# Streamed tiles at one offset within 256 bytes, weight sums on VectorE in the order of need, six raw buffers, and a ScalarE copy of one PSUM bank, in a two-layer diffusion backbone

## The chip, the core and the metric

The kernel runs on one core of a Trainium2 chip. The metric is the device time of one execution in microseconds (us). In what follows PE is the matrix engine (TensorE), PEld its weight loads, DVE is VectorE, ACT is ScalarE, POOL is GpSimd, and SP is the engine whose queue issues most of the DMAs.

## The reference

Two layers over 512 latent tokens x and 256 context tokens, width 1024. Each layer modulates and normalises, projects once, mixes tokens in three branches, gates and projects back, and ends in a SwiGLU feed-forward block (FFN) of hidden width 2816:

```python
for i in range(DEPTH):                      # DEPTH = 2
    hx = modulate(x, norm1_gain[i], mod_x[0], mod_x[1])
    zx = hx @ w_in[i]                       # 1024 -> q, k, v, pool, gating, 3 gates
    ...
    x = x + mod_x[2] * mixer_merge(zx, attn_x, *layer)
    x = x + mod_x[5] * swiglu(modulate(x, norm2_gain[i], mod_x[3], mod_x[4]),
                              w_ffn_in[i], w_ffn_out[i])
    if not last:                            # the context stream, same weights
        cx = cx + mod_c[2] * mixer_merge(zc, attn_c, *layer)
        cx = cx + mod_c[5] * swiglu(modulate(cx, ...), w_ffn_in[i], w_ffn_out[i])
return rmsnorm(x, final_gain)

def swiglu(h, w_in, w_out):
    gu = h @ w_in
    return (jax.nn.silu(gu[..., :D_FF]) * gu[..., D_FF:]) @ w_out
```

The outputs are fp32.

## The kernel before

**Matmuls.** Activations lie transposed in SBUF, features on the partitions and tokens along the free dimension. A fp32 product is made of three reduced-precision ones. Each operand is split into a high part and the rest: ACT writes the high part (names with `h`, as `wh_fo`), DVE the low part (`wl_fo`), and PE runs wh with the high activations, wl with the high ones and wh with the low ones (L321 to L323, and L1077 to L1079 in `product`). Raw weights come by DMA from SP's queue into 4 KB buffers (`rawp`, five of them), the split parts go to `hlp`. A matmul's operands stand in the profile as output, then moving activations, then weights. Moving operands are 512 columns wide for the x stream, 256 for the context stream, and 384 in the first layer's FFN.

**The first layer's FFN** (class `Seven`) takes both streams together, 768 tokens in two halves of 384. It uses a seven-product scheme for 2x2 blocks: the blocks of the activations are combined once into seven tiles B11, B21, T2, T1, T3, B22 and T4 (`norm`, `combine`; each split by ACT at L1022 and by DVE at L1023), and for each of 22 column pairs j of the weights DVE or POOL builds the sums S3, S1, S2 and S4 of the four weight blocks (L1098, L1100, L1102, L1104; S1, S2 and S4 are written over the raw tiles). A pair runs in four stages, A to D, each with its own split weights (`sg`, `sb`, `sc`, `su`):

- A: bank P gets B11, bank S gets B21. ACT copies P to m.
- B: P += T2, and ACT copies it to m6; bank R gets T1, and ACT copies it to m5.
- C: P += T3, and DVE adds it into m5 (L1188); R += B22, and DVE adds it into m6 (L1190).
- D: P += T4; the products of the halves become the hidden tile `fa` (L1197 to L1200).

A product is 12 matmuls of 384 columns. `chunk` follows every few pairs: the down projection into `pfo`, which DVE adds into X (L1221).

**Order.** The instructions of each engine are put in order by the tile framework from the order of the Python code, and each engine works through its own list. `Pipeline` keeps weight preparations two stages ahead of the matmuls that use them. Pairs 0 to 2 are begun early: their A products run while the other token half is still being normalised (`norm`, whose reciprocal root `rs_n2h` is a POOL instruction, L360, and whose row sums `ps_rbh` come from PE, L1033); for pairs 0 and 1 the four sums are POOL work, issued in `prep_a`. The FFN of the second layer and the mixers are ordinary matmuls on the `act` tiles; columns of the next layer's modulation (`mac`, `mq`, L250 to L253) are filled in between.

**Buffers.** Pools take SBUF in the order in which they are opened, so the size of each pool sets where the next one begins.

Of the kernel before, what the change touches and what calls it, by code (L numbers as in the profile page):

```python
# [19 lines left out]
P = 128  # L20
# [30 lines left out]
def hybrid_dit_kernel(ctx, tc, I, out):  # L51
# [4 lines left out]
    rawp = ctx.enter_context(tc.tile_pool(name="rawp", bufs=5))  # L56
    hlp = ctx.enter_context(tc.tile_pool(name="hlp", bufs=3))
    tmp = ctx.enter_context(tc.tile_pool(name="tmp", bufs=8))
    macp = ctx.enter_context(tc.tile_pool(name="macp", bufs=1))
    sml = ctx.enter_context(tc.tile_pool(name="sml", bufs=4))  # L60
    act = att = None
# [12 lines left out]
    def open_keys(l):  # L74
        nonlocal att
        kkp = zone("kkp", 1, "right")
        KK[:] = [kkp.tile([P, 2, CTX + SEQ], F32R, name=f"KK{l}{g}") for g in range(2)]
        att = zone("att", 2, "right")
# [327 lines left out]
    vtm = cst.tile([P, NT // P, P], F32, name="vtm")  # L406
# [579 lines left out]
    class Pipeline:  # L986
# [11 lines left out]

        def step(self):
            self.fill()  # L1000
            if not self.ready:
                return False
            do, w = self.ready.popleft()
            do(w)
            return True
# [3 lines left out]
    class Seven:  # L1009
# [38 lines left out]
        def combine(self):  # L1048

            b11, b21, b12, b22 = self.t  # L1050
            T2 = self.fap.tile([P, 4, HT], F32, tag="fa", name="T2")
            self.combo("T2")
            for h in (slice(0, 2), slice(2, 4)):
                V.tensor_tensor(b11[:, h], b12[:, h], b11[:, h], ALU.subtract)
                V.tensor_tensor(T2[:, h], b22[:, h], b11[:, h], ALU.subtract)
                self.split("T2", T2[:, h], h.start, h.stop)
                yield
            self.combo("T1")
            self.split("T1", b11, 0, 4)
            yield  # L1060
            V.tensor_tensor(b12, b22, b12, ALU.subtract)
            self.combo("T3")
            self.split("T3", b12, 0, 4)
            yield
            self.combo("B22")
            self.split("B22", b22, 0, 4)
            yield
            V.tensor_tensor(b21, b21, T2, ALU.subtract)
            self.combo("T4")
            self.split("T4", b21, 0, 4)  # L1070
# [10 lines left out]
        def pair(self, j, A, early=None):  # L1081
# [10 lines left out]
            def sums(which, eng=V):  # L1092
                g, u = d["g"], d["u"]
                a11, a12, a21, a22 = g[:, 0:4, :], g[:, 4:8, :], u[:, 0:4, :], u[:, 4:8, :]
                for x in which:
                    if x == 3:
                        d["S3"] = self.sp.tile([P, 4, P], F32, tag="S3", name=f"S3{j}")
                        eng.tensor_tensor(d["S3"], a11, a21, ALU.subtract)  # L1098
                    elif x == 1:
                        eng.tensor_tensor(a21, a21, a22, ALU.add)  # L1100
                    elif x == 2:
                        eng.tensor_tensor(a11, a21, a11, ALU.subtract)  # L1102
                    else:
                        eng.tensor_tensor(a12, a12, a11, ALU.subtract)  # L1104
# [12 lines left out]
            def prep_a():  # L1117
# [6 lines left out]
                elif early < 2:  # L1124
                    sums((3, 1, 2, 4), G)
                return w

            def prep_b():
                if early == 2:
                    sums((3, 1, 2))  # L1130
                w = parts("sb", d["g"][:, 0:4, :], d["u"][:, 0:4, :])
                if early in (None, 2):
# [3 lines left out]
            def prep_c():  # L1136
                return parts("sc", d["S3"], d["g"][:, 4:8, :])
# [48 lines left out]
            def run_c(w):  # L1186
                self.product(d["P"], w, 0, "T3", False)
                V.tensor_tensor(d["m5"], d["P"], d["m5"], ALU.add)  # L1188
# [16 lines left out]
    def ffn_seven(sv, streams, l, finish, mods):  # L1205
# [7 lines left out]
        def hidden(j):  # L1213
            t = sv.fap.tile([P, 2, NT], F32R, tag="fa", name=f"fa{l}{j}")
# [89 lines left out]
    rsc = cst.tile([P, 2], F32, name="rsc")  # L1304
# [3 lines left out]
    G.tensor_tensor(rsc, vc, half_neg[:, :2], ALU.pow)  # L1308
# [3 lines left out]
    def last_first(one, acc):  # L1312

        for i in range(2):
# [9 lines left out]
            if i == 0:  # L1324
                close("att", "kkp")
                seven.fap = zone("fap", 6, "right")
# [18 lines left out]
    seven.sp = zone("sp", 2)  # L1345
# [26 lines left out]
    pipe.fill(2)  # L1372
    for _ in range(3):
        pipe.step()
    run(seven.nx)
    cm = seven.combine()
    seven.late[0][0]()
    steps(cm, 2)
    for m, _ in seven.late[1:]:
        m()  # L1380
    for _, g in seven.late:
        g()
    run(cm)
    while pipe.step():
        pass
    close("sp", "cbp")
# [168 lines left out]
```

## Time and profile before

| | |
|---|---|
| median of 3 runs | 2111.31 us (2106.1 to 2111.85) |
| the profiled execution's own time | 2110.22 us |
| its span, first to last instruction | 2108.2 us |
| PE busy | 2014.7 us, 96% |
| PEld busy | 1721.2 us, 82% |
| DVE busy | 1287.2 us, 61% |
| ACT busy | 820.5 us, 39% |
| POOL busy | 444.7 us, 21% |
| mean granted TensorE clock | 0.986 |
| HBM traffic | 227.4 MB, 108 GB/s |

Busy time is the time in which an engine has at least one instruction at work; matmuls are pipelined, so two that follow each other overlap in the records, and the pace is read from start to start. The span lies 2.0 us under the run's own time. The clock is given as a share of 2.4 GHz, so 0.5 is 1.2 GHz.

### The profile page before, as it was taken

The page shows a single profiled execution, that of the slowest core. Times are in us where ns is not written, and L with a number is a line of the kernel's source. Part 1 is how long each engine was busy: PE and PEld are TensorE (multiplying, and loading weights), DVE is VectorE, ACT ScalarE, POOL GpSimd, SP SyncE. Part 2 cuts the span into 40 slices and gives each one's busy share as a digit, 9 for nine tenths or more (in the row PEclk, how much of TensorE's full clock was granted, in tenths as well). Part 3 has the DMA queues.
Part 4 walks back from the last instruction along what each step waited for, and adds up shares of the span by engine and source line. Part 5 has one row for each costly group of instructions (what it writes and reads, how often), then busy time and mean ns, then how long its engine had stood idle before and what let it go on. Part 6 is the DMA issues. An engine that isn't in the chain of part 4 may idle for free.

```text
span 2108.2 us, 28931 instructions
## 1 busy us (share of the span) xinstructions
PE 2014.7 (96%) x11423; PEld 1721.2 (82%) x11423; DVE 1287.2 (61%) x2014; ACT 820.5 (39%) x1400; POOL 444.7 (21%) x361
## 2 busy tenths in 40 slices
PE   6998999999999789999999999999999999999998
PEld 5988988777778779898989898777777788888886
DVE  4879628576774787665757545776755663343435
ACT  3655525343443534242525235453522342222223
POOL 3436302023773311010102012301211230000000
PEclk9999999999999899999999999999999999999999
DMA  9755733232553032232323123414246543333331
GB/s 299 212 162 158 209 90 94 66 100 69 177 165 110 11 110 70 85 94 68 95 60 110 52 89 91 115 51 125 61 125 195 170 120 102 98 90 99 92 94 47
DMA packets 326727, 233.47 MB, mean 111 GB/s; under 512 B 7680, under 2 KB 300720, under 8 KB 326592
## 3 DMA queue, kind: packets, MB, share of 16 engines
q1 hardware_dynamic: 323072, 226.78, 35.8%
q0 software_dynamic: 3280, 4.76, 1.1%
q8 instruction: 90, 1.47, 0.3%
q14 instruction: 45, 0.37, 0.1%
q10 hardware_dynamic: 240, 0.08, 0.0%
HBM read 225.30 MB, written 2.10 MB: 108 GB/s over the span
## 4 chain that ended last, share of the span: by engine, by line
PE 76%; DVE 13%; DMA 4%; issue 3%; ACT 3%; POOL 1%; ACTq 0%; POOLq 0%; DVEq 0%; SPq 0%
PE pfo L321 2%; PE pfo L323 2%; PE pP L1077 2%; PE pfo L322 2%; PE pP L1078 2%; PE pP L1079 2%; PE pfg1x L323 2%; PE pg1x L321 2%; PE pfu1x L323 2%; PE pfu1x L322 2%; PE pfu1x L321 2%; PE pfg1x L321 2%; PE pfg1x L322 2%; PE pg1x L322 2%; PE pg1x L323 2%
## 5 line engine op out<-in xcount | busy, mean ns | idle before, releaser
L251 POOL TENSOR_TENSOR mac<-mac,mq 128x512 f32<-128x512 f32 x84 | 133.6, 1590 | 270.5 <-ACT mq L250 266.8
L253 DVE SCALAR_TENSOR_TENSOR mac<-wm,scv,mac 128x512 f32<-128x512 f32 x140 | 132.4, 945 | 11.6 <-DMA wm<-in_w_mod_dram 9.3
L321 PE MATMUL pfo<-fa,wh_fo 128*128 128x512 f32 (+1 forms) x288 | 99.4, 348 | 9.7 <-DVE X L1221 9.5
L323 PE MATMUL pfo<-fa,wh_fo 128*128 128x512 f32 (+1 forms) x288 | 97.2, 338 | 0.0
L322 PE MATMUL pfo<-fa,wl_fo 128*128 128x512 f32 (+1 forms) x288 | 97.1, 337 | 0.0
L303 ACT ACTIVATE wh_fo<-raw_fo 128x1024 fp32r<-128x1024 f32 (+1 forms) x44 | 44.8, 1019 | 115.3 <-issue 111.2
L1221 DVE SCALAR_TENSOR_TENSOR X<-pfo,modv,X 128x256 f32<-128x256 f32 (+1 forms) x80 | 48.1, 614 | 62.2 <-PE pfo L323 61.8
L304 DVE TENSOR_TENSOR wl_fo<-raw_fo,wh_fo 128x1024 fp32r<-128x1024 f32 (+1 forms) x44 | 53.7, 1222 | 47.6 <-ACT wh_fo L303 47.4
L360 POOL TENSOR_TENSOR rs_fin<-v_fin,half_neg 128x1 f32<-128x1 f32 x4 | 3.1, 773 | 365.1 <-DVE v_fin L358 365.1
L321 PE MATMUL pg0x<-n1x0h,wh_g0x 128*128 128x512 f32 x192 | 76.3, 397 | 1.1 <-ACT tg0x L812 1.1
L322 PE MATMUL pg0x<-n1x0h,wl_g0x 128*128 128x512 f32 x192 | 76.0, 396 | 0.9 <-DVE wl_g0x L304 0.9
L321 PE MATMUL pg1x<-n1x1h,wh_g1x 128*128 128x512 f32 x192 | 76.9, 400 | 0.0
L322 PE MATMUL pg1x<-n1x1h,wl_g1x 128*128 128x512 f32 x192 | 76.3, 398 | 0.0
L323 PE MATMUL pg1x<-n1x1l,wh_g1x 128*128 128x512 f32 x192 | 76.2, 397 | 0.0
L323 PE MATMUL pg0x<-n1x0l,wh_g0x 128*128 128x512 f32 x192 | 75.8, 395 | 0.0
L321 PE MATMUL pfg1x<-n2x1h,wh_fg 128*128 128x512 f32 (+1 forms) x184 | 71.5, 388 | 0.8 <-ACT n2x1h L390 0.8
L323 PE MATMUL pfg1x<-n2x1l,wh_fg 128*128 128x512 f32 (+1 forms) x184 | 71.5, 388 | 0.5 <-POOL n2x1l L391 0.3
L321 PE MATMUL pfu1x<-n2x1h,wh_fu 128*128 128x512 f32 (+1 forms) x184 | 71.0, 386 | 0.0
L322 PE MATMUL pfu1x<-n2x1h,wl_fu 128*128 128x512 f32 (+1 forms) x184 | 70.9, 386 | 0.0
L322 PE MATMUL pfg1x<-n2x1h,wl_fg 128*128 128x512 f32 (+1 forms) x184 | 70.9, 385 | 0.0
L323 PE MATMUL pfu1x<-n2x1l,wh_fu 128*128 128x512 f32 (+1 forms) x184 | 70.9, 385 | 0.0
L321 PEld LDWEIGHTS pfo<-fa,wh_fo 128*128 128x128 f32 x288 | 54.3, 189 | 19.8 <-DVE X L1221 13.2
(799 smaller groups left out, 6589.0 us busy)
## 6 DMA issues: line engine op xcount, KB each, us to landing
wm<-in_w_mod_dram SPq DMA_DIRECT2D x96, 512.0 KB, 4.5
raw_fo<-in_w_ffn_out_dram SPq DMA_DIRECT2D x40, 512.0 KB, 3.4
raw_g0c<-in_w_in_dram SPq DMA_DIRECT2D x24, 512.0 KB, 4.6
raw_g0x<-in_w_in_dram SPq DMA_DIRECT2D x24, 512.0 KB, 3.8
raw_g1x<-in_w_in_dram SPq DMA_DIRECT2D x24, 512.0 KB, 4.0
raw_g<-in_w_ffn_in_dram SPq DMA_DIRECT2D x22, 512.0 KB, 4.0
raw_u<-in_w_ffn_in_dram SPq DMA_DIRECT2D x22, 512.0 KB, 4.0
raw_fg<-in_w_ffn_in_dram SPq DMA_DIRECT2D x22, 512.0 KB, 3.9
```

Of the source, the lines that this page charges most:

```text
L251: G.tensor_tensor(a, a, q, ALU.add)
L253: V.scalar_tensor_tensor(a, raw[:, k, :], sck, a, ALU.mult, ALU.add)
L303: S.activation(wh, raw_ap, AF.Copy)
L304: (eng or V).tensor_tensor(wl, raw_ap, wh.bitcast(F32), ALU.subtract)
L321: T_.matmul(ps, wh, H, start=first, stop=False)
L322: T_.matmul(ps, wl, H, start=False, stop=False)
L323: T_.matmul(ps, wh, L, start=False, stop=last)
L360: G.tensor_tensor(rs, v, half_neg[:, :nb], ALU.pow)
L1077: T_.matmul(ps, wh[:, k0 + k, :], H, start=first and k == 0, stop=False, skip_group_check=True)
L1078: T_.matmul(ps, wl[:, k0 + k, :], H, start=False, stop=False, skip_group_check=True)
L1079: T_.matmul(ps, wh[:, k0 + k, :], L, start=False, stop=k == 3, skip_group_check=True)
L1221: V.scalar_tensor_tensor(x, ps, modv[l][:, 40 + n, s.r:s.r + 1], x, ALU.mult, ALU.add)
```

## The change

**Buffer addresses.** The pool of small tiles is opened first; `rawp` has six buffers for five and `tmp` nine for eight; the tile `vtm` moves from the constants into the zone of the keys; `rsc` grows from 2 to 50 floats and a tile `line` of 192 bytes is added ahead of the `mac` tiles; the hidden tiles are divided over two zones, `fap` with four buffers and `fbp` with two. In the built programs the pools of matmul operands begin at these bytes of a partition (remainder by 256 in brackets), and every tile in them is a multiple of 256 bytes long:

| tiles | before | after |
|---|---|---|
| raw weights (`rawp`) | 35744 (160) | 33248 (224) |
| split weights (`hlp`) | 56224 to 76704 (160) | 57824 to 78304 (224) |
| `mac` tiles | 97696 (160) | 101600 (224) |
| activations and FFN blocks (`act`, `cbp`) | 102176 (32) | 105696 (224) |
| hidden tiles (`fap`, after also `fbp`) | (224) | (224) |
| keys | 217056 (224) | 217056 (224) |

So between a matmul's moving operand and its weights there were 128 bytes (modulo 256) in most matmuls and 64 in those of the first FFN's down projection; in the changed kernel there are none. The program has 8,633 such matmuls: 4,173 of 512 columns, 1,744 of 384 and 1,753 of 256 on `act` and `cbp` tiles, and 468 of 512 and 495 of 256 columns on hidden tiles of the first layer.

**Sums.** Pairs 0 and 1 have all their sums on DVE: S3, S1 and S2 ahead of stage B's split, S4 ahead of stage C's. S3 tiles come from `tmp` and no longer from a pool of their own. The start of the FFN interleaves `combine` with the weight preparations.

**Bank P after T3.** ACT copies it to a `tmp` tile s7, and DVE adds from there.

```diff
cst = ctx.enter_context(tc.tile_pool(name="cst", bufs=1))
-    rawp = ctx.enter_context(tc.tile_pool(name="rawp", bufs=5))
+    sml = ctx.enter_context(tc.tile_pool(name="sml", bufs=4))
+    rawp = ctx.enter_context(tc.tile_pool(name="rawp", bufs=6))
     hlp = ctx.enter_context(tc.tile_pool(name="hlp", bufs=3))
-    tmp = ctx.enter_context(tc.tile_pool(name="tmp", bufs=8))
+    tmp = ctx.enter_context(tc.tile_pool(name="tmp", bufs=9))
     macp = ctx.enter_context(tc.tile_pool(name="macp", bufs=1))
-    sml = ctx.enter_context(tc.tile_pool(name="sml", bufs=4))
-    act = att = None
+    act = att = vtm = None
+    macp.tile([P, 48], F32, tag="line", name="line")
     KK = []
...
     def open_keys(l):
-        nonlocal att
+        nonlocal att, vtm
         kkp = zone("kkp", 1, "right")
+        vtm = kkp.tile([P, NT // P, P], F32, name=f"vtm{l}")
         KK[:] = [kkp.tile([P, 2, CTX + SEQ], F32R, name=f"KK{l}{g}") for g in range(2)]
...
             G.tensor_tensor(acc[0], acc[0], q, ALU.add)
-    vtm = cst.tile([P, NT // P, P], F32, name="vtm")
     shuf = [(i + 16) % 32 for i in range(32)]
...
                 self.ready.append((item[1], item[0]()))
+        def go(self):
+            do, w = self.ready.popleft()
+            do(w)
+
         def step(self):
...
                 return False
-            do, w = self.ready.popleft()
-            do(w)
+            self.go()
             return True
...
             b11, b21, b12, b22 = self.t
-            T2 = self.fap.tile([P, 4, HT], F32, tag="fa", name="T2")
+            T2 = self.fbp.tile([P, 4, HT], F32, tag="fa", name="T2")
             self.combo("T2")
...
                     if x == 3:
-                        d["S3"] = self.sp.tile([P, 4, P], F32, tag="S3", name=f"S3{j}")
+                        d["S3"] = t2(f"S3{j}").rearrange("p (k n) -> p k n", k=4)
                         eng.tensor_tensor(d["S3"], a11, a21, ALU.subtract)
...
                     sums((2,))
-                elif early < 2:
-                    sums((3, 1, 2, 4), G)
                 return w
             def prep_b():
-                if early == 2:
+                if early is not None:
                     sums((3, 1, 2))
                 w = parts("sb", d["g"][:, 0:4, :], d["u"][:, 0:4, :])
-                if early in (None, 2):
+                if early is None:
                     sums((4,))
...
             def prep_c():
+                if early is not None:
+                    sums((4,))
                 return parts("sc", d["S3"], d["g"][:, 4:8, :])
...
                 self.product(d["P"], w, 0, "T3", False)
-                V.tensor_tensor(d["m5"], d["P"], d["m5"], ALU.add)
+                s7 = t2(f"s7{j}", HT)
+                S.activation(s7, d["P"], AF.Copy)
+                V.tensor_tensor(d["m5"], s7, d["m5"], ALU.add)
                 self.product(d["R"], w, 4, "B22", False)
...
         def hidden(j):
-            t = sv.fap.tile([P, 2, NT], F32R, tag="fa", name=f"fa{l}{j}")
+            t = (sv.fap if j % 6 < 4 else sv.fbp).tile([P, 2, NT], F32R, tag="fa", name=f"fa{l}{j}")
             A.append([t[:, 0, :], t[:, 1, :]])
...
     accc = mixer(SC, 0, *hs["c"], mid=early, then=lambda: fill.add(latents()), done=first)
-    rsc = cst.tile([P, 2], F32, name="rsc")
+    rsc = cst.tile([P, 50], F32, name="rsc")
     V.tensor_copy(ssc, token_ss(SC, accc, "n2c0"))
...
     V.tensor_scalar(vc, ssc, 1.0 / D, EPS, ALU.mult, ALU.add)
-    G.tensor_tensor(rsc, vc, half_neg[:, :2], ALU.pow)
+    G.tensor_tensor(rsc[:, :2], vc, half_neg[:, :2], ALU.pow)
     seven = Seven(0)
...
                 close("att", "kkp")
-                seven.fap = zone("fap", 6, "right")
+                seven.fap = zone("fap", 4, "right")
                 half_ss(0)
...
     seven.cbp = zone("cbp", 7)
-    seven.sp = zone("sp", 2)
+    seven.fbp = zone("fbp", 2, "right")
     accs = {"c": [], "x": []}
...
             next(seven.nx)
-    pipe.fill(2)
+    pipe.fill(3)
     for _ in range(3):
-        pipe.step()
+        pipe.go()
     run(seven.nx)
     cm = seven.combine()
-    seven.late[0][0]()
+    for m, _ in seven.late:
+        m()
     steps(cm, 2)
-    for m, _ in seven.late[1:]:
-        m()
+    pipe.fill(1)
+    next(cm)
+    pipe.fill(2)
     for _, g in seven.late:
         g()
+    pipe.go()
+    next(cm)
+    pipe.fill(2)
+    next(cm)
+    pipe.go()
+    pipe.fill(2)
+    pipe.go()
     run(cm)
...
         pass
-    close("sp", "cbp")
+    close("cbp", "fbp")
     open_act()
...
```

POOL at the start of the first FFN (`sq_m0x` is the sum of squares that the normalisation needs, `raw_g00` and `raw_u00` are the raw weights of pair 0). Before:

```order
L859 TENSOR_TENSOR sq_m0x0_6509<-sq_m0x0_6509,sqxo6_6833 128x2x128
L1098 TENSOR_TENSOR S30_6910<-raw_g00_6902,raw_u00_6904 128x512
L1098 TENSOR_TENSOR S31_6932<-raw_g01_6924,raw_u01_6926 128x512
L1100 TENSOR_TENSOR raw_u00_6904<-raw_u00_6904 128x512
L1100 TENSOR_TENSOR raw_u01_6926<-raw_u01_6926 128x512
L1102 TENSOR_TENSOR raw_g00_6902<-raw_u00_6904,raw_g00_6902 128x512
L360 TENSOR_TENSOR rs_n2h1_6917<-v_n2h1_6915,half_neg_93 128x2
L1104 TENSOR_TENSOR raw_g00_6902<-raw_g00_6902 128x512
```

After:

```order
L860 TENSOR_TENSOR sq_m0x0_6510<-sq_m0x0_6510,sqxo6_6834 128x2x128
L362 TENSOR_TENSOR rs_n2h1_6913<-v_n2h1_6911,half_neg_94 128x2
L249 TENSOR_SCALAR mac101_7270<-wm100_7271,scv_131 128x512
L253 TENSOR_TENSOR mac101_7270<-mac101_7270,mq1001_7276 128x512
L253 TENSOR_TENSOR mac101_7270<-mac101_7270,mq1020_7309 128x512
```

The eight sums are gone from POOL, and `rs_n2h1` follows the squares at once.

DVE at the same start, from the last normalised tiles on (`th`: normalised tokens, cbT2 and cbT1: the split blocks T2 and T1, `wl_sb0`: the low part of pair 0's stage-B weights). Before:

```order
L1055 TENSOR_TENSOR T2_7066<-th11_7039,th00_6802 128x768 x2
L1174 TENSOR_TENSOR g10_7080<-pS01_6945,m0_7064 128x384
L1023 TENSOR_TENSOR cbT2_7067<-T2_7066,cbT2_7067 128x768
L1174 TENSOR_TENSOR g11_7083<-pS01_6945,m1_7076 128x384
L1174 TENSOR_TENSOR g12_7086<-pS2_7013,m2_7078 128x384
L1023 TENSOR_TENSOR cbT2_7067<-T2_7066,cbT2_7067 128x768
L1023 TENSOR_TENSOR cbT1_7089<-th00_6802,cbT1_7089 128x1536
```

After:

```order
L1059 TENSOR_TENSOR T2_7049<-th11_7018,th00_6803 128x768 x2
L1102 TENSOR_TENSOR S30_7059<-raw_g00_6903,raw_u00_6905 128x512
L1027 TENSOR_TENSOR cbT2_7050<-T2_7049,cbT2_7050 128x768
L1104 TENSOR_TENSOR raw_u00_6905<-raw_u00_6905 128x512
L1027 TENSOR_TENSOR cbT1_7069<-th00_6803,cbT1_7069 128x1536
L1027 TENSOR_TENSOR cbT2_7050<-T2_7049,cbT2_7050 128x768
L1106 TENSOR_TENSOR raw_g00_6903<-raw_u00_6905,raw_g00_6903 128x512
L1117 TENSOR_TENSOR wl_sb0_7064<-raw_u00_6905,wh_sb0_7063 128x512
L1102 TENSOR_TENSOR S31_7072<-raw_g01_6920,raw_u01_6922 128x512
L1117 TENSOR_TENSOR wl_sb0_7064<-raw_g00_6903,wh_sb0_7063 128x512
```

The sums of pairs 0 and 1 stand between the splits, the low parts of stage B's weights behind them; before, those low parts stood ahead of these rows, between the rows that normalise.

A pair in the middle of the FFN, where bank P of pair 5 is emptied after T3: ACT (first fence before, second after).

```order
L1180 ACTIVATE m65_7895<-pP5_7848 128x384
L1184 ACTIVATE m55_7910<-pR5_7897 128x384
L1112 ACTIVATE wh_sg6_7919<-raw_g06_7912 128x1024
L1112 ACTIVATE wh_sb6_7951<-raw_g06_7912 128x512
L1112 ACTIVATE wh_sb6_7951<-raw_u06_7914 128x512
```

```order
L1184 ACTIVATE m65_7906<-pP5_7859 128x384
L1188 ACTIVATE m55_7921<-pR5_7908 128x384
L1116 ACTIVATE wh_sg6_7930<-raw_g06_7923 128x1024
L1193 ACTIVATE s75_7947<-pP5_7859 128x384
L1116 ACTIVATE wh_sb6_7964<-raw_g06_7923 128x512
```

And DVE there, before and after:

```order
L1113 TENSOR_TENSOR wl_su5_7880<-raw_u05_7779,wh_su5_7879 128x512
L1113 TENSOR_TENSOR wl_sg6_7920<-raw_g06_7912,wh_sg6_7919 128x1024
L1188 TENSOR_TENSOR m55_7910<-pP5_7848,m55_7910 128x384
L1102 TENSOR_TENSOR raw_g06_7912<-raw_u06_7914,raw_g06_7912 128x512
L1104 TENSOR_TENSOR raw_g06_7912<-raw_g06_7912 128x512
L1190 TENSOR_TENSOR m65_7895<-pR5_7897,m65_7895 128x384
```

```order
L1117 TENSOR_TENSOR wl_su5_7891<-raw_u05_7788,wh_su5_7890 128x512
L1102 TENSOR_TENSOR S36_7927<-raw_g06_7923,raw_u06_7925 128x512
L1104 TENSOR_TENSOR raw_u06_7925<-raw_u06_7925 128x512
L1117 TENSOR_TENSOR wl_sg6_7931<-raw_g06_7923,wh_sg6_7930 128x1024
L1194 TENSOR_TENSOR m55_7921<-s75_7947,m55_7921 128x384
L1106 TENSOR_TENSOR raw_g06_7923<-raw_u06_7925,raw_g06_7923 128x512
```

ACT has one row more, `s75<-pP5`; on DVE the row that read `pP5` reads `s75`, and the sums S36 and `raw_u06` stand just ahead of `wl_sg6`, where before they stood seventeen rows further up, in pair 4's stages.

## Rows read from the trace of the kernel before

**Rows 1.** The page: PE, and a group (busy, mean ns, idle before).

```profile
PE 2014.7 (96%) x11423; PEld 1721.2 (82%) x11423; DVE 1287.2 (61%) x2014; ACT 820.5 (39%) x1400; POOL 444.7 (21%) x361
...
L304 DVE TENSOR_TENSOR wl_fo<-raw_fo,wh_fo 128x1024 fp32r<-128x1024 f32 (+1 forms) x44 | 53.7, 1222 | 47.6 <-ACT wh_fo L303 47.4
```

**Rows 2.** Waits of PE: us in total, times, longest.

```profile
PE pP L1077 <- DVE m L1188: 12.1, 7, 2.9
PE pfo L321 <- DVE X L1221: 9.5, 7, 3.4
PE ps_rbh L1033 <- POOL rs_n2h L360: 9.0, 1, 9.0
```

**Rows 3.** Timeline of POOL (start, us, instruction, idle before), FFN start.

```profile
700.66 3.47 POOL L1098 TENSOR_TENSOR S<-raw_g,raw_u 128x512 f32<-128x512 f32 x2
...
710.18 1.42 POOL L360 TENSOR_TENSOR rs_n2h<-v_n2h,half_neg 128x2 f32<-128x2 f32 x1
```

**Rows 4.** Timeline of DVE at the same start.

```profile
702.92 0.15 DVE L358 TENSOR_SCALAR v_n2h<-ps_ssh 128x2 f32<-128x2 f32 x1
...
705.14 6.76 DVE L1023 TENSOR_TENSOR cbB<-th,cbB 128x768 fp32r<-128x768 f32 x4
```

**Rows 5.** Timeline of PE there: two starts after an idle time.

```profile
711.64 0.79 PE L1033 MATMUL ps_rbh<-ident,rs_n2h 128*128 128x128 f32 x2 [9.05 <-POOL rs_n2h L360]
...
729.48 0.69 PE L1077 MATMUL pP<-cbT,wh_sb 128*128 128x384 f32 x1 [2.94 <-ACT cbT L1022]
```

**Rows 6.** Busy us of PE, PEld, DVE, ACT, POOL; clock; DMA, by stretch.

```profile
714.00:729.40 15.40, 12.53 (x69) 12.20 (x67) 11.18 (x22) 10.64 (x23) 2.55 (x2) 0.94 0.01 2
729.40:770.20 40.80, 36.57 (x181) 34.11 (x182) 35.14 (x47) 23.29 (x38) 8.30 (x6) 0.93 0.26 82
923.10:926.50 3.40, 3.40 (x13) 3.40 (x12) 3.40 (x7) 2.42 (x6) 0.00 (x0) 0.51 0.00 0
```

**Rows 7.** Timeline of DVE, FFN start: one instruction of each size.

```profile
729.79 0.95 DVE L1023 TENSOR_TENSOR cbT<-T,cbT 128x768 fp32r<-128x768 f32 x1
...
732.46 1.76 DVE L1023 TENSOR_TENSOR cbT<-th,cbT 128x1536 fp32r<-128x1536 f32 x1
...
744.14 0.69 DVE L1113 TENSOR_TENSOR wl_sc<-S,wh_sc 128x512 fp32r<-128x512 f32 x1
```

**Rows 8.** Timeline of DVE around a wait for bank P.

```profile
917.48 1.58 DVE L1098 TENSOR_TENSOR S<-raw_g,raw_u 128x512 f32<-128x512 f32 x1 [4.15 <-DMA raw_u<-in_w_ffn_in_dram]
...
921.18 0.55 DVE L1188 TENSOR_TENSOR m<-pP,m 128x384 f32<-128x384 f32 x1
```

**Rows 9.** Timeline of PE around that wait.

```profile
918.86 0.33 PE L1079 MATMUL pR<-cbB,wh_sc 128*128 128x384 f32 x1
921.78 0.44 PE L1077 MATMUL pP<-cbT,wh_su 128*128 128x384 f32 x1 [2.59 <-DVE m L1188]
```

**Rows 10.** Timeline of ACT: a copy of a bank.

```profile
725.22 0.46 ACT L1170 ACTIVATE m<-pP 128x384 f32<-128x384 f32 x1
```

**Rows 11.** Pace: first and last of 429 matmuls of 512 columns.

```profile
1800.09 0.40 PE L323 MATMUL pfo1x<-fa,wh_fo 128*128 128x512 f32 x1
...
1899.95 0.40 PE L322 MATMUL pfu1x<-n2x1h,wl_fu 128*128 128x512 f32 x1
```

**Rows 12.** Pace: first and last of 23 of the down projection.

```profile
859.17 0.40 PE L322 MATMUL pfo<-fa,wl_fo 128*128 128x512 f32 x1
...
864.22 0.39 PE L323 MATMUL pfo<-fa,wh_fo 128*128 128x512 f32 x1
```

**Rows 13.** Next weights at the moving operand's offset: two matmuls.

```profile
440.63 0.40 PE L323 MATMUL pg0x<-n1x0l,wh_g0x 128*128 128x512 f32 x1
440.87 0.28 PE L535 MATMUL s0x<-KK,Q0x 128*128 128x256 f32 x1
...
444.61 0.40 PE L323 MATMUL pb0x<-y20xl,wh_b0x 128*128 128x512 f32 x1
444.85 0.34 PE L535 MATMUL s0x<-KK,Q0x 128*128 128x384 f32 x1
```

## The prediction

> **What bounds the kernel now.** I read the page first. PE is busy for 96% of the span [rows 1], no other engine comes near, and the chain that ended last is mostly PE. So time can be won in two ways only: PE waits less, or each matmul takes less. Then the list of PE's waits [rows 2]. Its three largest entries are a wait for bank P in the first layer's FFN (12.1 us in 7 places), one for the down projection's bank (9.5 us, which no edit touches), and one wait of 9.0 us at the start of that FFN. The timelines of the start [rows 3 to 5] and of one wait for bank P [rows 8, 9] say what each waits for; the clock and the idle time come from a table by stretch [rows 6]; the pace of matmuls from the first and the last start of long series [rows 11, 12].
>
> **Start of the FFN.** PE's 9.05 us before `ps_rbh` [rows 5] end with `rs_n2h` on POOL at 710.18, though its input was written by 703.07 [rows 4]: five of the eight sums stood ahead of it from 700.66 on [rows 3]. In the new order the reciprocal root follows the squares directly, so it ends at about 704.5 and PE resumes some 7 us earlier. What is late next is DVE. After `v_n2h` it has one `wl_sg`, four halves of `cbB` and another `wl_sg`. These ran beside POOL's sums, the four halves taking 6.76 us [rows 4]; a split of 128x768 without POOL takes 0.95 [rows 7] and one of 128x1024 on average 1.22 [rows 1]. That is 2 x 1.2 + 4 x 0.95 = 6.2, so they end near 709.1. The normalising rows up to T2 follow: in 714.0 to 729.4 DVE was busy for 11.18 us [rows 6], of which four rows of 0.69 [rows 7] were low parts of stage B, which now come later; 8.4 remain, so T2 is there at about 717.5. Between T2 and PE's second matmul of stage B the new order puts six rows of 128x512, two of 128x768 and one of 128x1536, that is 6 x 0.69 + 2 x 0.95 + 1.76 = 7.8, less some 0.07 by which neighbouring rows overlap: 7.2. Stage B then runs from about 724.8 instead of 729.48 [rows 5], a gain of 4.6. So the wait of 9.05 gives about half back: a new idle stretch of about 7 us stands between A and B. From B's start to the first down projection, 40.8 us with PE busy for 36.57 [rows 6], 4.2 us are idle; they are waits for weights whose sums now come in the order of need, and I count them as won. Together -9. Bounds: -4, if those 4.2 stay because DVE has taken over eight sums (5.5 us of 0.69 each), and -12, if the first stage B loses less to the lowered clock.
>
> **Bank P.** In the example DVE stands for 4.15 us in front of `S`, waiting for the DMA of `raw_u`, and behind it are `wl_sg` and the addition that empties bank P, which begins at 921.18 [rows 8]; PE, done with C at 918.86 plus one pace, begins D at 921.78 [rows 9]. Six of the seven waits have this form, 11.4 of the 12.1 us; the seventh lies in the start above. After the three longest the clock is granted at 0.51 for 3.4 us, as in the row of 923.10 [rows 6]; at half pace about half of the work of such a stretch is lost, 1.5 us, so 4.6 for three. With the change two things remove the wait. ACT empties the bank and does not stand behind the sum; its copy costs 0.46 [rows 10], and stage C's other product, 12 matmuls of 0.176, gives it 2.1 us of cover. And `S` stands seventeen rows later on DVE, close to its use, so it seldom meets a DMA in flight. What can still stop PE is `wl_sg`, late by what is left of the same DMA. Together -11.4 - 4.6 = -16; I take -15, with -8 and -16 as bounds. The 22 copies take 22 x 0.46 = 10.1 us of ACT, hidden, since ACT is busy for 39% [rows 1]; if that cover were gone, each stage C would pay its 0.46.
>
> **Buffers and order.** The sixth raw buffer lets a load start one tile earlier; PE's waits for raw weights beyond those above are small, so 0, within 2 either way. `S3` and `s7` are two more users of `tmp` in each pair: six tiles of nine where it was four of eight.
>
> **One offset for all streams.** This edit concerns the pace of 8,633 matmuls, so one nanosecond on each is 8.6 us. Three prices can be read. First, today's: 512 columns with moving operand and weights 128 bytes apart take (1899.95 - 1800.09)/428 = 233.3 ns [rows 11]; in the down projection, 64 apart, (864.22 - 859.17)/22 = 229.5 [rows 12]. Why these differ by 3.8 ns the trace cannot say: the distance, or the moving operand's own offset, 224 against 32. If it is the own offset, all move to the quicker pace. Second, the trace has ten matmuls during which weights at the very offset of the moving operand were loaded, which is what the change makes of all: the five of 512 columns took 229 to 240 ns, mean 235 (two of them, at 240 each, are in [rows 13]), which is 1.7 to 1.9 ns above today's; those of 256 columns were some 1.7 above theirs. But they end a series and the next matmul is of another kind, so they are weak evidence. Third, no effect: most matmuls stay as they are, and the 468 wide ones of the down projection lose their 3.8 ns, 1.8 us. Between -22 and +16 I take the third, since a difference of 2% in pace between two kinds of matmul has no proven cause here, and the two signs stand against each other.
>
> On this edit a page of the Trainium skill speaks: "SBUF — State Buffer", section "SBUF: two separate sides", says that PE's own ports to SBUF never wait on anyone, and that weight loads have an independent read port. By it an address offset changes nothing and the sum stays at its other terms. The trace shows a pace that differs by 3.8 ns between two kinds of equal size, which that rule alone does not explain.
>
> **The sum.** The profiled execution took 2110.2 us, 1.1 under the median of its three runs. 2110.2 - 9 - 15 = 2086; with the third price of the offset, +2: **2088**.
>
> **The rivals.**
>
> *Quicker pace.* The moving operand's own offset sets the 229.5 ns. Then the 4,173 wide matmuls gain 3.8 each (15.9 us) and the 1,744 of 384 columns perhaps as much (6.6): 2086 - 22 = 2064. For it: both kinds have the same shape, engine and weights' offset, and only the moving operand differs. Against it: the distance differs as well.
>
> *Somewhat slower pace.* Equal offsets cost what the mean of the ten matmuls says, 1.9 ns: 8,633 x 1.9 = 16, so 2102. For it: the three offsets then stand in a plausible row. Against it: ten matmuls at the end of their series.
>
> *Clearly slower pace, the other side.* A read of the moving operand and a load of weights at one offset collide each time, as in the two at 240 ns. That is 6.7 ns on 4,641 matmuls of 512 columns, and in proportion, from 2 to 4.5, on the narrower ones: 31 + 8 + 5 = 44 us, so 2130. It decides from 24/8,633 = 2.8 ns per matmul on: there the offset eats both other gains; beyond 3.5 the kernel is measurably slower.
>
> *The waits come back.* `tmp` holds nine tiles of which a pair uses six, a pair and a half in place of two; a sum then waits for an older tile and DVE stands again in front of bank P's work or `wl_sg`. That takes the 15 back: 2101.
>
> **Chances.** No effect of the offset 0.44, quicker pace 0.26, somewhat slower 0.15, waits back 0.06, clearly slower 0.09. The likeliest gives 2088, and its own range, from the bounds of the two large terms (-4 and -12, -8 and -16) and 2 us for buffers, is 2082 to 2102. For 8 in 10 the range reaches to most of the quicker case and to the somewhat slower one: 2060 to 2106. About 0.3% (6.3 us) is what a measurement of this kernel can tell from no change. Faster by more: all of the first two cases but a little, and two thirds of the third and fourth, 0.80. Within 0.3%: the rest of those and a part of the clearly slower case, where the price lies between 2 and 3.5 ns, 0.12. Slower: 0.08.
>
> **What would show it.** In the trace of the changed kernel: `rs_n2h` on POOL within 2 us of `v_n2h`; PE's wait for it under 2.5 us and a new idle time of 5 to 8 us ahead of stage B; no entry for bank P above 2 us among PE's waits; a half-clock stretch less at three places around 923, 1025 and 1124; 512-column series at 233 ns (229.5 in the quicker case, 235 in the slower one). The prediction is wrong if the pace leaves 231 to 234.5, or if `wl_sg` or a tile of `tmp` takes the place of the wait for bank P.

## The result

The changed kernel takes 2079.9 us (median of four runs, 2075.35 to 2084.49) against 2111.06 of the kernel before: ratio 0.9857, 95% interval 0.9831 to 0.9884, so 31 us less. It lies inside the range, 8 us under the forecast of 2088. The profiled execution has a span of 2078.4 us and took 2080.25.

PE is still the bound; the page's line of busy times answers to [rows 1]:

```profile
PE 1989.9 (96%) x11423; PEld 1719.4 (83%) x11423; DVE 1290.7 (62%) x2022; ACT 830.4 (40%) x1422; POOL 428.1 (21%) x353
```

PE is busy for 24.8 us less than before, with the same 11,423 instructions, while its idle time (the span less PE's busy time) went from 93.5 to 88.5: most of the gain is in the matmuls themselves, not in the waits. First and last start of series, in the second layer's FFN (442 matmuls, answering to [rows 11]) and in the first layer's down projection (23, [rows 12]):

```profile
1780.02 0.39 PE L324 MATMUL pfo1x<-fa,wl_fo 128*128 128x512 f32 x1
...
1879.98 0.39 PE L324 MATMUL pfu1x<-n2x1h,wl_fu 128*128 128x512 f32 x1
```

```profile
846.86 0.39 PE L324 MATMUL pfo<-fa,wl_fo 128*128 128x512 f32 x1
...
851.87 0.39 PE L325 MATMUL pfo<-fa,wh_fo 128*128 128x512 f32 x1
```

That is 99.96/441 = 226.7 ns for 233.3, and 5.01/22 = 227.7 for 229.5.

The waits of PE, answering to [rows 2] (us in total, times, longest):

```profile
PE pfo L323 <- DVE X L1227: 11.5, 5, 4.7
...
PE pP L1081 <- ACT wh_sb L1116: 5.5, 2, 4.7
...
PE pP L1081 <- ACT m L1174: 5.2, 4, 1.3
...
PE s1x L536 <- ACT pr1x L549: 3.3, 1, 3.3
...
PE ps_rbh L1037 <- POOL rs_n2h L362: 2.0, 1, 2.0
```

The wait for bank P behind DVE's addition is gone from the list and the one for `rs_n2h` fell from 9.0 to 2.0 us. New are two for ACT in the FFN (`wh_sb`, `m`) and one in the second layer's attention (`s1x`).

The start of the FFN, POOL, DVE and PE (answering to [rows 3 to 5]):

```profile
697.34 1.63 POOL L362 TENSOR_TENSOR rs_n2h<-v_n2h,half_neg 128x2 f32<-128x2 f32 x1 [2.17 <-DVE v_n2h L360]
```

```profile
697.10 0.16 DVE L360 TENSOR_SCALAR v_n2h<-ps_ssh 128x2 f32<-128x2 f32 x1 [0.65 <-PE ps_ssh L1345]
697.18 1.23 DVE L1117 TENSOR_TENSOR wl_sg<-raw_g,wh_sg 128x1024 fp32r<-128x1024 f32 x1
698.32 3.56 DVE L1027 TENSOR_TENSOR cbB<-th,cbB 128x768 fp32r<-128x768 f32 x4
```

```profile
699.02 0.84 PE L1037 MATMUL ps_rbh<-ident,rs_n2h 128*128 128x128 f32 x4 [1.96 <-POOL rs_n2h L362]
...
718.50 0.69 PE L1081 MATMUL pP<-cbT,wh_sb 128*128 128x384 f32 x1 [4.69 <-ACT wh_sb L1116]
```

`rs_n2h` begins 0.1 us after its input is written and is done at 698.97; the four halves of `cbB` take 3.56 us where they took 6.76 beside POOL's sums. The new idle time ahead of stage B is 4.7 us. From the last row sums of the normalisation (701.77 before, 696.23 now) to stage B it was 27.7 us and is 22.3. The first down projection follows 39.8 us later, where it was 40.7 [rows 5, 6]: nearly nothing was won there.

Which load DVE waited for changed too. Before:

```profile
DVE S L1098 <- DMA raw_u<-in_w_ffn_in_dram: 33.1, 14, 4.1
...
DVE mac L253 <- DMA wm<-in_w_mod_dram: 9.3, 5, 3.1
```

After:

```profile
DVE mac L255 <- DMA wm<-in_w_mod_dram: 22.6, 8, 4.6
```

Waits for `raw_u` were 33.1 us in 14 places and are gone; those for `wm`, the modulation weights of the filler work, grew from 9.3 to 22.6.

### The profile page after: what moved, and what is told of

The parts are those of the page before. It is cut to its first block, busy times and chain, and to the rows that moved or that the text cites. A ratio compares the mean times of both kernels' runs of the same rounds, so it can differ in the third digit from the quotient of the medians.

```text
span 2078.4 us, 28922 instructions
## 1 busy us (share of the span) xinstructions
PE 1989.9 (96%) x11423; PEld 1719.4 (83%) x11423; DVE 1290.7 (62%) x2022; ACT 830.4 (40%) x1422; POOL 428.1 (21%) x353
## 4 chain that ended last, share of the span: by engine, by line
PE 76%; DVE 13%; ACT 3%; issue 2%; DMA 2%; POOL 2%; SPq 1%; ACTq 0%; POOLq 0%; DVEq 0%
PE pfo L323 2%; PE pfo L325 2%; PE pfo L324 2%; PE pP L1081 2%; PE pP L1082 2%; PE pP L1083 2%; PE pfg1x L325 2%; PE pg1x L323 2%; PE pfu1x L324 2%; PE pfu1x L325 2%; PE pfu1x L323 2%; PE pfg1x L323 2%; PE pfg1x L324 2%; PE pg1x L324 2%; DMA wm<-in_w_mod_dram 2%
## 5 line engine op out<-in xcount | busy, mean ns | idle before, releaser
L255 DVE SCALAR_TENSOR_TENSOR mac<-wm,scv,mac 128x512 f32<-128x512 f32 x140 | 131.8, 942 | 25.0 <-DMA wm<-in_w_mod_dram 22.6
```

Source lines behind the costliest of these rows:

```text
L255: V.scalar_tensor_tensor(a, raw[:, k, :], sck, a, ALU.mult, ALU.add)
```

## Experiments: the offsets

**The layout alone.** The kernel before, with all streams at 224; every engine keeps its order.

```diff
+    macp.tile([P, 32], F32, tag="line", name="line")
...
-    rsc = cst.tile([P, 2], F32, name="rsc")
+    rsc = cst.tile([P, 18], F32, name="rsc")
...
```

> The kernel before with 64 bytes added to rsc and a tile of 128 bytes ahead of the mac tiles, so that the activations, the raw and split weights and the hidden tiles all begin at 224 modulo 256; every engine keeps its order. Theory 1 (the offsets carry most of the gain): about 25 us less than before, some 2086, with 512-column series at 227 ns instead of 233, 384 columns at 173.7, 256 columns about 1 ns slower; waits as before. Rival (the offsets bring little, the quicker pace seen in the changed kernel comes with the other edits): 2105 or more and series still at 233 ns.

Measured: 2092.8 us, ratio 0.9911 (0.9891 to 0.9932), so 14 to 23 us less than before. Here and below a ratio is to the kernel before run in the same set; its median was 2112.3 us in this set and 2109.7 and 2108.6 in the later ones. The 512-column series are at 226.7 ns. The offsets are most of the change's gain.

**The layout undone, in three ways.** Only the two pads of the changed kernel are altered, so that the order of all instructions stays. In the first, moving operands are at 96 and weights at 224; in the second at 224 and 160; in the third both at 32.

```diff
-    macp.tile([P, 48], F32, tag="line", name="line")
+    macp.tile([P, 80], F32, tag="line", name="line")
```

> The changed kernel with its extra tile 128 bytes longer: activations and FFN blocks begin at 96, weights stay at 224, so the two are 128 bytes apart as before the change; order unchanged. Theory 1 (the distance between moving operand and weights sets the pace): 512 columns back to 233 ns, 384 to 175.9, in all some 2104. Rival (the moving operand's own offset, 32 being the slow one, sets it): 512 columns stay near 227 to 229 ns, 2080 to 2090.

```diff
-    macp.tile([P, 48], F32, tag="line", name="line")
+    macp.tile([P, 64], F32, tag="line", name="line")
...
-    rsc = cst.tile([P, 50], F32, name="rsc")
+    rsc = cst.tile([P, 34], F32, name="rsc")
```

> The changed kernel with raw and split weights at 160 and all moving operands at 224, so 64 bytes apart, as only the first down projection had it before. Theory 1 (distance): 512 columns at 229.3 ns and 256 columns at 117.4, so about +8 us on the wide ones and -5 on the narrow ones: 2083. Rival (own offset of the moving operand): 512 columns at 227.2 as in the changed kernel, 2080; 256 columns at 119.8.

```diff
-    rsc = cst.tile([P, 50], F32, name="rsc")
+    rsc = cst.tile([P, 66], F32, name="rsc")
```

> The changed kernel with activations, raw and split weights at 32, so no distance between them; hidden tiles of the first FFN stay at 224, 64 bytes apart the other way round. Theory 1 (distance): as the changed kernel, 227.2 ns at 512 columns, 2080. Rival (own offset): moving operands at 32 give 232.9 ns again, some 2104.

Measured: 2099.7 (0.9947, 0.9928 to 0.9965), 2082.2 (0.986, 0.9834 to 0.9885) and 2080.8 us (0.9858, 0.9839 to 0.9877). First and last start of a long 512-column series of the first (429 matmuls) and of the third (441):

```profile
1780.05 0.39 PE L325 MATMUL pfo1x<-fa,wh_fo 128*128 128x512 f32 x1
...
1879.92 0.39 PE L324 MATMUL pfu1x<-n2x1h,wl_fu 128*128 128x512 f32 x1
```

```profile
1780.18 0.39 PE L323 MATMUL pfo1x<-fa,wh_fo 128*128 128x512 f32 x1
...
1879.91 0.39 PE L325 MATMUL pfu1x<-n2x1l,wh_fu 128*128 128x512 f32 x1
```

99.87/428 = 233.3 ns at a distance of 128 with a moving operand at 96, and 99.73/440 = 226.7 at a distance of 0 with one at 32, the offset that the rival had called slow. So the distance decides, not the operand's own place; the second kernel says the same from the other side, with moving operands at 224 as in the changed kernel and yet 229.1 ns. The single gaps of such a series differ too. At 0 all of them lie between 225 and 228 ns; at 128 they alternate strictly, 229 or 230 and 237 or 238, in the kernel before and in the first of the three; at 64 they repeat in threes, about 226, 229 and 232. Mean start-to-start times of undisturbed neighbours, from the traces of five kernels (ns; matmuls of each cell in brackets):

| moving operand's offset less the weights', modulo 256 | 512 columns | 384 columns | 256 columns |
|---|---|---|---|
| 0 (224/224, changed kernel) | 227.2 (4,164) | 173.7 (1,761) | 119.8 (1,736) |
| 0 (32/32) | 227.2 (4,162) | 173.7 (1,767) | 119.7 (1,741) |
| 64 (224/160) | 229.1 (4,165) | 173.4 (1,751) | 116.3 (1,710) |
| 128 (32/160, before) | 232.9 (4,173) | 175.9 (1,744) | 118.8 (1,753) |
| 128 (96/224) | 232.9 (4,171) | 175.9 (1,763) | 118.7 (1,728) |
| 192 (224/32, down projection) | 233.3 (456) | | 115.9 (487) |

The best distance depends on the width: 0 at 512 columns, 64 or 192 at 256. At 384, 0 and 64 are alike and 128 is the slow one. For the change this makes 5.7 x 4,173 + 2.2 x 1,744 - 1.0 x 1,753 = 23.8 + 3.8 - 1.8, and about 1 x 468 - 2 x 495 = -0.5 us for the down projection: 25 us by the paces. These counts, and the 8,633 of "The change", are of undisturbed neighbours alone; the traces record 9,144 such matmuls (4,320, 1,848 and 1,920, and 528 of either width in the down projection).

By the runs it is 20, both with the layout alone (2112.3 - 2092.8) and with it undone (2099.7 - 2079.9). The profiles show where the other 5 us stay. With the layout alone PE is busy for 25.2 us less than before (1989.5 for 2014.7), and idle for 4.1 more (97.6 for 93.5); with the layout undone in the changed kernel it is busy for 22.6 us more (2012.5) and idle for 3.0 less (85.5 for 88.5). So the pace is won in full, and where PE comes sooner to an engine that is late, a part goes into waiting.

## Experiments: the sums, the copy, the buffers

**The copy of bank P alone**, on the kernel before.

```diff
-                V.tensor_tensor(d["m5"], d["P"], d["m5"], ALU.add)
+                s7 = t2(f"s7{j}", HT)
+                S.activation(s7, d["P"], AF.Copy)
+                V.tensor_tensor(d["m5"], s7, d["m5"], ALU.add)
```

> The kernel before with only the copy of bank P by ScalarE after T3 (tmp stays at eight buffers, S3 in its own pool). Theory 1 (VectorE is late there for a load it waits for, and the copy only moves what PE waits for next): the 12 us of waits for bank P go, but some two thirds comes back as waits for wl_sg or for the copy of bank P to m, so about 4 us less than before, some 2107. Rival (the prediction's step): the waits go and nothing takes their place, about 15 us less, 2096.

Measured: 2105.9 us beside 2109.7, ratio 0.9981 (0.9965 to 0.9997). What PE waits for instead, and what DVE waits for:

```profile
PE pP L1077 <- ACT m L1170: 5.3, 5, 1.3
```

```profile
DVE S L1098 <- DMA raw_u<-in_w_ffn_in_dram: 33.4, 13, 4.8
```

DVE stands as long as ever in front of `raw_u`, and 5.3 us of waiting turn up one stage on, where ACT copies bank P to m; another 2.2 are for `wl_sg`, and those for the down projection's bank grew from 9.5 to 11.6. In all PE is idle for 93.3 us where it was 93.5: the copy moved the 12 us of waits and won none of them. What it won is clock. The three stretches at 0.51 behind the longest waits (one of them in [rows 6]) are gone, and through the middle of the FFN the clock is granted in full, in the row by stretch at 1.00:

```profile
781.00:1180.00 399.00, 382.90 (x2179) 357.05 (x2179) 263.37 (x398) 152.39 (x265) 40.13 (x26) 1.00 0.28 82
```

PE is busy for 5.2 us less (2009.5 for 2014.7), about the 4.6 that the prediction had set for the clock. So the copy bought 4 us, not 15.

**The sums and the start alone**, on the kernel before.

```diff
-                elif early < 2:
-                    sums((3, 1, 2, 4), G)
...
-                if early == 2:
+                if early is not None:
                     sums((3, 1, 2))
...
```

> The kernel before with only the sums of pairs 0 and 1 on VectorE and the new start sequence. Theory 1: the 9 us in front of ps_rbh fall to 2, but a longer idle time ahead of stage B and waits of pair 2 give part of it back: 5 us less, some 2106. Rival (the prediction's step): 9 us less, 2102; or, if VectorE's eight extra sums cost more than the wait, no change.

Measured: 2102.7 us beside 2109.7, ratio 0.9963 (0.9946 to 0.9979): 7 us, between the two expectations and compatible with both.

**Five raw buffers in the changed kernel.**

```diff
-    rawp = ctx.enter_context(tc.tile_pool(name="rawp", bufs=6))
+    rawp = ctx.enter_context(tc.tile_pool(name="rawp", bufs=5))
```

> The changed kernel with five raw buffers again; all offsets stay as they are. Theory 1 (the sixth buffer is what lets raw_u land in time, the loads of the modulation weights being what VectorE waits for now): VectorE waits for raw_u again, 3 to 8 us more than the changed kernel, 2083 to 2088. Rival (the order of need alone does it, the sixth buffer is idle): same as the changed kernel, 2080.

Measured: 2076.3 us (2071.72 to 2079.66), ratio 0.9836 (0.9802 to 0.987), no slower than with six. There is no wait for `raw_u` here either, so it was not the sixth buffer that removed it but the later place of `S` in DVE's order. Which edit moved `S` there was not run alone: with the layout, the copy or the sums alone the waits for `raw_u` stayed at 32.0, 33.4 and 33.1 us, which leaves the S3 tiles from `tmp` with its ninth buffer, or several edits together. The waits for `wm` are 10.7 us instead of 22.6, and of PE's, those for `m` are 1.2 instead of 5.2 and that for `s1x` is gone:

```profile
DVE mac L255 <- DMA wm<-in_w_mod_dram: 10.7, 5, 2.6
```

The sixth buffer earns nothing in this kernel.

**The modulation weights one step ahead.** In the changed kernel DVE meets the `wm` load in flight, four times in the FFN and once in the attention. One of the four; the timelines of DVE, ACT and PE:

```profile
1005.39 0.75 DVE L255 SCALAR_TENSOR_TENSOR mac<-wm,scv,mac 128x512 f32<-128x512 f32 x1 [4.63 <-DMA wm<-in_w_mod_dram]
1006.06 1.78 DVE L1104 TENSOR_TENSOR raw_u<-raw_u 128x512 f32<-128x512 f32 x1
1007.76 2.31 DVE L1117 TENSOR_TENSOR wl_sg<-raw_g,wh_sg 128x1024 fp32r<-128x1024 f32 x1
```

```profile
1014.11 0.63 ACT L1116 ACTIVATE wh_sc<-raw_g 128x512 fp32r<-128x512 f32 x1 [0.75 <-DVE raw_g L1108]
...
1015.47 0.47 ACT L1174 ACTIVATE m<-pP 128x384 f32<-128x384 f32 x1
```

```profile
1010.12 0.45 PE L1082 MATMUL pP<-cbB,wl_sg 128*128 128x384 f32 x1 [1.31 <-DVE wl_sg L1117]
...
1015.99 0.44 PE L1081 MATMUL pP<-cbT,wh_sb 128*128 128x384 f32 x1 [1.29 <-ACT m L1174]
```

DVE stands for 4.63 us in front of `mac`, the sums and `wl_sg` come late, PE waits 1.31 us for `wl_sg`; ACT then waits for a sum (`wh_sc`), its copy of bank P stands behind that, and PE waits another 1.29. In the second layer's attention the same load holds up a softmax:

```profile
1450.96 1.54 DVE L255 SCALAR_TENSOR_TENSOR mac<-wm,scv,mac 128x512 f32<-128x512 f32 x2 [4.25 <-DMA wm<-in_w_mod_dram]
1452.41 1.28 DVE L545 TENSOR_REDUCE sm1x<-s1x 128x1 f32<-128x512 f32 x2
```

```profile
1454.74 0.69 PE L536 MATMUL s1x<-KK,Q1x 128*128 128x384 f32 x1 [3.31 <-ACT pr1x L549]
```

Before, that `mac` stood behind the softmax in DVE's order; here it stands ahead, and PE loses 3.31 us and runs on at the lower clock, in the row by stretch (busy us of five engines, granted clock) at 0.60:

```profile
1455.00:1462.00 7.00, 7.00 (x26) 5.69 (x27) 4.37 (x15) 2.86 (x9) 0.00 (x0) 0.60 0.31 95
```

The experiment puts one filler step between a load and its use. The load stays at its step; the work on it, on DVE, ACT and POOL, comes one step later than before:

```diff
                 raw = rawp.tile([P, 2, 512], F32, tag="raw", name=f"wm{l}{u}{k2}")
...
+                yield
                 for r, a in enumerate(acc):
...
-                for _ in range(stride):
+                for _ in range(stride - 1):
                     yield
```

> The changed kernel with the modulation weights (wm) loaded one filler step ahead of the work on them. Theory 1 (what is left of the predicted gain is lost to VectorE standing in front of a wm load, four times in the first FFN for 3.3 to 4.6 us and once in the second layer's attention): PE's waits for wh_sb, m and s1x behind those go, 5 to 12 us less than the changed kernel, 2068 to 2075. Rival (a wm buffer held one step longer makes raw weights late instead): same or slower, 2080 to 2090.

Measured: 2059.6 us (2056.09 to 2062.05), ratio 0.9752 (0.9726 to 0.9778): 20 us less than the changed kernel, more than expected. DVE's waits for loads and PE's longest waits:

```profile
DVE mac L256 <- DMA wm<-in_w_mod_dram: 5.9, 4, 4.3
...
DVE S L1103 <- DMA raw_u<-in_w_ffn_in_dram: 0.3, 1, 0.3
```

```profile
PE pfo L324 <- DVE X L1228: 8.1, 6, 3.2
PE ps_mod L264 <- POOL mac L254: 7.1, 5, 3.4
...
PE s1x L537 <- ACT pr1x L550: 3.4, 1, 3.4
```

The waits for `m` are gone. The two profiles differ by 24 us; 14 of them are less idle time of PE (74.6 for 88.5) and 10.5 less busy time (1979.4 for 1989.9), with a mean granted clock of 0.992 for 0.986. Compared at equal places in PE's order, about 6 come from the context stream's layer, 7 from the start of the FFN and 13 from the rest of it; some 1 us was lost between the first two, where PE now waits for `mac` on POOL. The wait of `s1x` stayed (3.4), so the attention was not mended by this, against what I expected; DVE still meets the load in flight there:

```profile
1426.87 1.54 DVE L256 SCALAR_TENSOR_TENSOR mac<-wm,scv,mac 128x512 f32<-128x512 f32 x2 [4.32 <-DMA wm<-in_w_mod_dram]
```

**The same with five buffers, and without the other edits.** The first takes one buffer from that kernel; the second has the layout and the early `wm` loads only, on the kernel before.

> The changed kernel with the modulation weights one filler step ahead and five raw buffers. Theory 1 (the sixth buffer is idle as long as wm is loaded late, but pays once wm holds a buffer one step longer): 3 to 8 us more than with six, 2063 to 2068. Rival (the sixth buffer does nothing): 2060.

> The kernel before with the offsets of all streams at 224 and the modulation weights one filler step ahead; without the sums on VectorE, the copy and the sixth buffer. Theory 1 (the copy and the new start are worth what they were alone, 4 and 7 us, and early loads remove VectorE's waits behind them): some 11 to 15 us more than with all edits, 2071 to 2075. Rival (early loads alone remove the waits for bank P, the copy is worth nothing then): about 7 us more, 2067.

Measured: 2067.3 (0.9801, 0.9774 to 0.9828) and 2071.7 us (0.9822, 0.9797 to 0.9847). With five buffers DVE's wait for `wm` is back, and so is PE's for `m`:

```profile
DVE mac L256 <- DMA wm<-in_w_mod_dram: 27.5, 13, 3.0
```

```profile
PE pP L1082 <- ACT m L1175: 5.6, 5, 1.2
```

So the sixth buffer is worth 8 us once `wm` holds a buffer for longer, and the sums, the copy and that buffer together 12. That leaves about 4 for the sums and the copy, which alone gave 7 and 4.

The kernel with five buffers also says that the chain shown above is not the whole of the 20 us. DVE waits longer for `wm` there than in the changed kernel (27.5 us for 22.6, though in shorter pieces) and PE as long for `m` (5.6 for 5.2), and yet it is 13 us quicker. The chain of waits can account for the 8 us that the sixth buffer adds. For the 13 the later place of the work in each engine's order is the obvious rival, and no run tells it from shorter waits.

**Another distance for the context stream.** In the changed kernel, and in the one with early `wm` loads, the context's weights are moved by 64 bytes, so that its 256-column matmuls have the distance 192; `tmp` gives up a buffer for it.

```diff
...
+    def half(nm, kt, n):
+        o = 16 if re.search(r"\dc|first", nm) else 0
+        return [hlp.tile([P, 1088], F32R, tag=f"W{x}", name=f"w{x.lower()}_{nm}")[:, o:o + kt * n]
+                .rearrange("p (k n) -> p k n", n=n) for x in "HL"]
...
-        wh = hlp.tile([P, kt, n], F32R, tag="WH", name=f"wh_{nm}")
-        wl = hlp.tile([P, kt, n], F32R, tag="WL", name=f"wl_{nm}")
+        wh, wl = half(nm, kt, n)
...
```

> The changed kernel with the split weights of the context stream's products 64 bytes further in their buffers, so that those 256-column matmuls have moving operand and weights 192 bytes apart, and the wide ones still 0; tmp has eight buffers for nine, to make room. Theory 1 (distance sets the pace, and its best value differs with the width): the some 1,450 matmuls of the context stream fall from 119.7 to 115.9 ns, 5 to 6 us less than the changed kernel, 2074. Rival (115.9 was a property of the down projection alone): they stay at 119.7, 2080.

> The changed kernel with the modulation weights one filler step ahead and the context stream's weights 192 bytes from the moving operand. Theory 1 (the two are independent): 2059.6 less 5 to 6, some 2054. Rival (the gain of either hides the other's, or eight tmp buffers cost it): 2058 or more.

Measured: 2076.0 (0.984, 0.982 to 0.986) and 2058.6 us (0.9754, 0.9732 to 0.9777). The pace follows the distance, 115.4 ns (1,381 matmuls) for 119.8. The time of the first is 4 us under the changed kernel, with overlapping ranges; of the second nothing is left to see beside the 2059.6 without this edit: in its first 514 us PE is busy for 5.7 us less (479.2 for 484.8) and idle for as much more. The quickest kernels are the two with early `wm` loads and six buffers, 2.5% under the kernel before.

## Why the prediction held, point by point

The number was right by luck: two errors, 13 us too much and 22 us too little, cancelled for the most part. The forecast had 24 us from the waits and -2 from the offsets; the runs show some 11 (ratio 0.9947 with the offsets undone, by its interval 7 to 15) and 20.

- **What bounds the kernel**: right. PE kept 96%, and only its waits and its pace counted.
- **Start of the FFN, -9**: the first half was right and close. `rs_n2h`, the rest of its wait and DVE as the next late engine came as worked out; stage B gained 5.4 for 4.6 forecast, and the new idle time ahead of it is 4.7 for some 7. The second half, 4.2 us of idle time between B and the first down projection, was wrong: it stayed, because the last of the early pairs now waits for its own sums on DVE: they run there from 739.95 us on, and PE stands for 2.6 us at 744 to 747 for `wh_sb` and `wl_sb`, the split parts made from them. Alone these edits gave 7.
- **Bank P, -15**: the failed step. The wait went, as said, but the sentence on what could still stop PE treated it as small. DVE was late because it stood in front of a load, and taking one consumer off its path leaves the others: ACT's copies and the weights' low parts, which wait for DVE's sums. Alone the edit left PE's idle time as it was (93.3 us for 93.5): of the -16 the 11.4 of waits came to nothing, and what is left is about the 4.6 of clock. In the changed kernel the three half-clock stretches are gone too, as forecast, but others came, as the one at `s1x`, and the mean granted clock is 0.986 as before. That the new order takes `S` out of the way of `raw_u` was right; the next load in the order, `wm`, took its place, and I had not looked at it, though it stood in the list of DVE's waits with 9.3 us.
- **Buffers, 0**: right for this kernel, in which five buffers do no worse; the sixth earns its 8 us only when `wm` holds a buffer for longer.
- **Offsets, +2**: the wrong case was taken as likeliest. The rival "quicker pace" had about the right total, 22 us, and the wrong cause, the moving operand's own offset; the experiment with moving operand and weights both at 32 excludes that, and the wide series went below its 229.5 ns. The ten matmuls that pointed to a slower pace at equal offsets misled; they stood next to another kind of matmul, as the prediction said, but that this is the reason is not shown. The forecast of 231 to 234.5 ns for the wide series, named as what would prove it wrong, was missed with 226.7.
- **The page cited there**: at 512 columns the runs show 5.7 ns of 233 that hang on addresses alone. The Trainium skill, "SBUF — State Buffer", section "SBUF: two separate sides", has PE's own ports never waiting on anyone; by it, as the prediction read it, the offsets would have given nothing, and here the measurement decides.
- **The second layer's attention** was in no term: 3.3 us of new waiting, since the order of filler work shifted there.

## What to carry to other kernels

When PE waits for an engine, follow that engine's queue to what it waits for itself; an edit that routes around it pays only what the next consumer of the same engine does not take back, and in the copy's case that was all of the waiting, and only the clock gained. Load filler weights a step ahead of their use and give them a buffer for it: here that was worth two thirds of what the whole change brought, though how much of it is the load's time to land and how much the new order is not shown. And where thousands of like matmuls run back to back, the distance between the moving operand and the weights is worth one cheap run per value, for each width by itself.

## What the runs showed of the hardware

The pace of fp32r matmuls in series depends on the distance modulo 256 bytes between moving operand and weights, and on nothing else of their place that was tried: at 512 columns 227.2, 229.1, 232.9 and 233.3 ns for 0, 64, 128 and 192 (the last from the down projection alone), at 256 columns 119.8, 116.3, 118.8 and 115.9. At 512 columns and a distance of 128 the mean of a long series is made of gaps of some 229 and 237 ns in strict turn, although the matmuls of a product come in threes; at 0 all gaps are 225 to 228. Why the two widths rank the distances differently stays open, as do all distances in between, which were not tried.
